# Head-masked X, fp32r rank products and a written TensorE order in the scans of an RWKV-7/gMLP step

## The chip, the core and the metric

The kernel runs on one core of one Trainium2 chip. The metric is the device time of one execution in microseconds (us): the median of three runs before the change is 3405.29 (3395.33 to 3405.65). Times in the text beside it come from one profiled execution of the kernel before.

## The reference

One inference layer of a flow-matching backbone over 640 tokens of width 2048 (128 of context, 512 of a latent grid): adaLN modulation, w_in, on half of the channels a bidirectional RWKV-7 scan and on the other half a chunked gMLP, w_out, a SwiGLU feed-forward network (FFN) and a last RMSNorm. What the change touches is this:

```python
def _delta_scan(r, w, k, v, aa, bb, s0, reverse):
    def step(S, inp):
        r_t, w_t, k_t, v_t, a_t, b_t = inp
        sa = jnp.einsum('bhvk,bhk->bhv', S, a_t)
        S = S * w_t[:, :, None, :] + sa[..., None] * b_t[:, :, None, :] + v_t[..., None] * k_t[:, :, None, :]
        return S, jnp.einsum('bhvk,bhk->bhv', S, r_t)
...
    wt = jnp.tanh(wd)
    for d in range(2):
        w_log = -jax.nn.softplus(-(lp['w0'][d] + wt @ lp['w2'][d])) - 0.5
        decay = heads(jnp.exp(-jnp.exp(w_log)))
        a = jax.nn.sigmoid(lp['a0'][d] + ad @ lp['a2'][d])
        kd = heads(k * (1.0 + (a - 1.0) * lp['k_a']))
        y, s_fin = _delta_scan(rh, decay, kd, vh, -kk, kk * heads(a), s0[:, d], reverse=(d == 1))
        out = out + _group_norm(y, lp['gn_w'], lp['gn_b']) \
            + jnp.sum(rh * kd * lp['r_k'], axis=-1, keepdims=True) * vh
    o = out.reshape(B, T, D_A) * gate
...
    x = x + g1 * (jnp.concatenate([o_a, o_b], axis=-1) @ lp['w_out'])
```

There are 16 heads of 64 channels, two directions d, and a rank of 64 for `wt @ w2` and `ad @ a2` (the rank products).

## The kernel before, in words

Channels lie on the 128 partitions, tokens along the free axis in two halves of 320 (HALF). Every large product is made in fp32r, in three passes: each operand is split into a rounded part hi and a remainder lo, and hi x hi, hi x lo and lo x hi are added up in one PSUM bank (`win` L185 to L187, `wout` L999 to L1001, w_out's first half L1382 to L1384). `split` (L163 and L164) makes hi on ScalarE and lo on VectorE from each weight block of 128x512 that SP's queue has loaded.

The first long stage multiplies h by w_in, block by block. Generators ride between its passes, with budgets that a `Mixer` hands out: for each of eight pairs of heads `take_r`, `take_v` and `take_k`. `take_k` prepares the scan in chunks of 64 tokens, ten per direction. Its rank products (pwa, L562) are plain fp32 matmuls of 64 rows: wl holds w2 in the lower and a2 in the upper 64 partitions, and wa holds tanh(wd) and ad likewise (`low_rank`, L483 and L484). From the decays and keys VectorE makes R and X (X in four operations, L606 to L610); pG (L624) multiplies X by R for each chunk and head in fp32, 64 rows a head, the two heads in turn. The transposes pXT (L641), the first W (pW0, L652) and `solve` with its blocks of 32x32 follow. w_mod's products (pm, L869) run in the same stage. Everything that the scans need goes through DRAM (d_S).

The second stage holds the scans. w_out's second half (`wout_b`) needs only the gMLP's output and gives TensorE something to do: eight of its 32 blocks come first, the rest lies between the scans' steps. A hop is a turn of a loop (117 in all); pair p starts at hop 13p (OFF), and two pairs are under way at a time. `recur(p)` takes one yield a phase, three phases a step: w (L1117) and the outputs y of the step ahead (L1083, L1088), then u (L1132), then s (L1153), from which VectorE makes the new state SN (L1157 to L1160). Each is four small matmuls for each of two chains (latent and context), in a bank of its own for each chain: two banks for w, s and swap, one for u, two for y, from which ScalarE copies Y with its sum (L1102). `finish(p)` then normalises Y over the heads (GpSimd L1182 and L1192), joins the two directions by matmuls with I and J (pO, L1200) and applies the gate (pmm, L496); a second Mixer deals it out in pieces. On every engine the instructions stand in the order that the scheduler picks, from the order of the code and its own costs.

After the scans, w_out's first half runs through 16 blocks for each half of the tokens, in two banks of pbig and two of pb2 in turn, each block with its eight row blocks of o on end. The FFN follows.

Of the kernel before, what the change touches and what calls it, by code (L numbers as in the profile page):

```python
# [10 lines left out]
F32 = mybir.dt.float32  # L11
# [8 lines left out]
P = 128  # L20
# [31 lines left out]
LAG = 4  # L52
LAST_LAG = 3
ROWO = 4
RAWB = 13
WTAIL = 8
OFF = 13
MB = 6
# [26 lines left out]
def flow_step(ctx: ExitStack, tc, x_prompt, x_sample, state_rwkv, c, c_ctx, w_mod, b_mod,  # L85
# [279 lines left out]
    wa = bk.tile([P, T], F32, name="wa", bufs=1)  # L365
# [132 lines left out]


# [25 lines left out]
    def take_k(pr, p):  # L525
# [26 lines left out]
        for d in range(2):  # L552
# [5 lines left out]
            for hf in range(2):  # L558
                s = slice(HALF * hf, HALF * hf + HALF)
                two = [pk.tile([P, HALF], F32, tag="g", name="pwa") for _ in range(2)]  # L560
                for h in range(2):
                    TE.matmul(two[h], wl[hsl(h), d, :], wa[hsl(h), s], start=True, stop=True)  # L562
# [42 lines left out]
            X = bz.tile([P, NCH, 2, CH], F32, tag="X", name="X", bufs=1)  # L605
            V.tensor_mul(rev(X[0:64, :, 1, :]), v3(tha)[0:64], i3[0:64])  # L606
            V.tensor_mul(rev(X[64:128, :, 0, :]), v3(tha)[64:128], i3[64:128])
            yield 1.5
            V.tensor_mul(rev(X[0:64, :, 0, :]), v3(f)[0:64], i3[0:64])
            V.tensor_mul(rev(X[64:128, :, 1, :]), v3(f)[64:128], i3[64:128])  # L610
# [8 lines left out]
            for (c0, c1) in ((0, 4), (4, 8), (8, NCH)):  # L619
                two = [pk.tile([P, 4, P], F32, tag="g", name="pG") for _ in range(2)]  # L620
                for cc in range(c0, c1):
                    for h in range(2):
                        s = hsl(h)
                        TE.matmul(two[h][:, cc - c0, :], X[s, cc, :, :].rearrange("p s t -> p (s t)"),  # L624
                                  R[s, cc, :, :].rearrange("p s t -> p (s t)"), start=True, stop=True)
# [10 lines left out]
            for (c0, c1) in ((0, 8), (8, NCH)):  # L636
                two = [pk.tile([P, 8, CH], F32, tag="g", name="pXT") for _ in range(2)]
                for cc in range(c0, c1):
                    for h in range(2):
                        s = hsl(h)  # L640
                        TE.transpose(two[h][:, cc - c0, :], X[s, cc, :, :].rearrange("p s t -> p (s t)"), ident[s, s])  # L641
# [373 lines left out]
    with ExitStack() as ph:  # L1015
        rw = ph.enter_context(tc.tile_pool(name="rw", bufs=1))
        sm = ph.enter_context(tc.tile_pool(name="sm", bufs=2))
        pws = ph.enter_context(tc.tile_pool(name="pws", bufs=2, space=PSUM))
        pu = ph.enter_context(tc.tile_pool(name="pu", bufs=1, space=PSUM))
# [32 lines left out]

        def swap(src):
            ps = pws.tile([P, 2, CH], F32, tag="ws", name="swap")
            for d in range(2):
                for h in range(2):
                    TE.matmul(ps[hsl(h), d, :], src[hsl(h), d, :], I2[hsl(h), :], start=True, stop=True)
            o = sm.tile([P, 2, CH], F32, tag="ST", name="ST", bufs=7)
            V.tensor_copy(o, ps)
            return o  # L1060

        def recur(p):
# [7 lines left out]
            yield 1  # L1070
            late = []

            def outputs():
                if not late:
                    return


                ys = [py.tile([P, 2, CH], F32, tag=f"y{d}", name="y_ps") for d in range(2)]

                def states(e, r, ST, **kw):  # L1080
                    for d in range(2):
                        for h in range(2):
                            TE.matmul(ys[d][hsl(h), e, :], r[hsl(h), d, F_R + CH:F_R + P], ST[hsl(h), d, :], **kw)  # L1083

                def chunk(e, r, **kw):
                    for d in range(2):
                        for h in range(2):
                            TE.matmul(ys[d][hsl(h), e, :], r[:, d, F_G + CH * h:F_G + CH * h + CH],  # L1088
                                      r[:, d, F_Z + CH * h:F_Z + CH * h + CH], **kw)

                for e, (cc, r, ST) in enumerate(late):
                    if ST is None:
                        chunk(e, r, start=True, stop=True)
                    elif e == 0:
                        states(e, r, ST, start=True, stop=False)
                        chunk(e, r, start=False, stop=True)
                    else:
                        chunk(e, r, start=True, stop=False)
                        states(e, r, ST, start=False, stop=True)
                for e, (cc, r, ST) in enumerate(late):  # L1100
                    for d in range(2):
                        S.activation(u.Y[:, d, cc[d], :], ys[d][:, e, :], AF.Copy, accum_out=u.ys[:, d, cc[d]:cc[d] + 1])  # L1102
# [3 lines left out]
            for step in range(len(LATC)):  # L1106
                act = [c for c in chains if step < len(seqs[c[0]])]
                Ws = []
                for ctx_, ST in act:
                    r = recs[p, ctx_, step]  # L1110
# [3 lines left out]
                    w_ps = pws.tile([P, 2, CH], F32, tag="ws", name="w_ps")  # L1114
                    for d in range(2):
                        for h in range(2):
                            TE.matmul(w_ps[osl(h), d, :], r[hsl(h), d, F_R:F_R + CH], ST[hsl(h), d, :],  # L1117
                                      start=True, stop=True)
                    W = sm.tile([P, 2, CH], F32, tag="W", name="W", bufs=4)
                    for h in range(2):  # L1120
                        q = osl(h)
                        V.tensor_add(W[q], w_ps[q], r[q, :, F_Z + CH * h:F_Z + CH * h + CH])
                    Ws.append(W)
                outputs()
                yield 1
                for (ctx_, ST), W in zip(act, Ws):
                    r = recs[p, ctx_, step]
                    ups = pu.tile([P, 2, CH], F32, tag="u", name="u_ps")
                    for d in range(2):
                        for h in range(2):  # L1130
                            q = osl(h)
                            TE.matmul(ups[q, d, :], r[q, d, F_T:F_T + CH],  # L1132
                                      r[q, d, F_Z + CH * h:F_Z + CH * h + CH] if W is None else W[q, d, :],
                                      start=True, stop=True)
                    V.tensor_copy(r[0:64, :, F_Z + CH:F_Z + P], ups[0:64])
                    S.copy(r[64:128, :, F_Z:F_Z + CH], ups[64:128])
                yield 1
                for ch in act:
                    ctx_, ST = ch
                    cc = seqs[ctx_][step]  # L1140
                    r = recs.pop((p, ctx_, step))
                    late.append((cc, r, ST))
                    if step + 1 == len(seqs[ctx_]) and not ctx_:
                        continue
                    s_ps = pws.tile([P, 2, CH], F32, tag="ws", name="s_ps")
                    SN = sm.tile([P, 2, CH], F32, tag="ST", name="SN", bufs=7)
                    ge = gend[:, p].rearrange("p d c -> p (d c)")[:, flip(cc)].unsqueeze(2)
                    if ST is not None:
                        SG = sm.tile([P, 2, CH], F32, tag="SG", name="SG", bufs=4)
                        V.tensor_tensor(out=SG, in0=ST, in1=ge.to_broadcast([P, 2, CH]), op=ALU.mult)  # L1150
                    for d in range(2):
                        for h in range(2):
                            TE.matmul(s_ps[hsl(h), d, :], r[:, d, F_X + CH * h:F_X + CH * h + CH],  # L1153
                                      r[:, d, F_Z + CH * h:F_Z + CH * h + CH], start=True, stop=True)
                    for d in range(2):
                        if ST is None:
                            V.tensor_scalar_mul(SN[:, d, :], s_ps[:, d, :], ge[:, d])  # L1157
# [756 lines left out]
```

## Time and profile before

| what | us |
|---|---|
| median of three runs | 3405.29 |
| the profiled execution | 3410.02 |
| its span | 3408.2 |
| modulation and the first blocks (0 to 150) | 150 |
| w_in with rank products, pG, solve (150 to 1203) | 1053 |
| first blocks of w_out's second half (1203 to 1242) | 39 |
| scans (1242 to 1537) | 295 |
| the last pair's normalisation (1537 to 1560) | 23 |
| w_out's first half (1560 to 1690) | 130 |
| FFN and the end (from 1690) | 1718 |

The stages are read from the first and last instruction of their matmul lines, to a microsecond or so. The profile gives for each engine the time in which it worked, and for TensorE the clock that was granted (1.00 is full). PE is TensorE's matmuls, PEld its weight loads, DVE VectorE, ACT ScalarE, POOL GpSimd, SP the engine that issues most DMAs. A matmul's shape reads rows in use * columns in use. The profiled execution was 4.7 us longer than the median.

### The profile page before, as it was taken

The numbers are of one execution on the slowest core, as the hardware profiler recorded it, in microseconds if no ns is written. First come the engines' busy times: TensorE is split into PE (matmuls) and PEld (weight loads), VectorE is DVE, ScalarE is ACT, GpSimd is POOL, SyncE is SP. The second block draws the span as 40 slices with busy tenths as digits, with TensorE's granted clock in tenths as the row PEclk, the third lists the DMA queues.
The fourth block names the chain that finished last, engine by engine and source line by source line (L and its number), as shares of the span: only waits on it lengthen the run. The fifth ranks groups of instructions, "written<-read, shape, count | busy, mean of one in ns | idle before, by whom it ended". The sixth has DMA issues, their size and how long they took to land.

```text
span 3408.2 us, 72541 instructions
## 1 busy us (share of the span) xinstructions
PE 3249.5 (95%) x28216; PEld 2934.2 (86%) x28216; DVE 2411.4 (71%) x4320; ACT 1450.7 (43%) x3161; POOL 1263.0 (37%) x1112
## 2 busy tenths in 40 slices
PE   6899999999999999998899999999999999999996
PEld 3688777777877887777889999999999999999996
DVE  4547666756866766664887777777777787877787
ACT  3334443433434434333564444444444445443365
POOL 0001122111212103322336565656656555555543
PEclk8999999889999999999999999999999999999998
DMA  8766776566677677654543434344343455543553
GB/s 321 233 188 185 184 189 170 154 171 179 186 186 180 170 226 231 209 163 145 173 124 103 130 114 122 114 126 122 111 123 121 129 165 165 158 138 115 154 163 115
DMA packets 736208, 550.11 MB, mean 161 GB/s; under 512 B 140360, under 2 KB 670040, under 8 KB 727032
## 3 DMA queue, kind: packets, MB, share of 16 engines
q1 hardware_dynamic: 723544, 531.78, 52.5%
q0 software_dynamic: 9984, 13.13, 1.8%
q8 instruction: 222, 3.64, 0.4%
q14 instruction: 122, 1.00, 0.1%
q10 hardware_dynamic: 2336, 0.57, 0.1%
HBM read 436.68 MB, written 111.28 MB: 161 GB/s over the span
## 4 chain that ended last, share of the span: by engine, by line
PE 76%; DVE 11%; issue 4%; DMA 4%; POOL 2%; ACT 2%; SPq 0%; DVEq 0%; ACTq 0%; POOLq 0%
PE P L1529 15%; PE P L1527 14%; PE P L1528 14%; PE big L185 4%; PE big L187 4%; PE big L186 4%; PE pG L624 3%; PE pm L869 2%; PE big L999 2%; DMA raw<-in_w_in_dram 1%; DVE lo L1330 1%; DMA wt<-in_w_mod_dram 1%; PE big L1382 1%; PE big L1384 1%; PE pmm L496 1%
## 5 line engine op out<-in xcount | busy, mean ns | idle before, releaser
L1529 PE MATMUL P<-xo,lo 128*128 128x320 f32 x2352 | 728.1, 310 | 2.3 <-DVE lo L1330 2.2
L1527 PE MATMUL P<-xo,hi 128*128 128x320 f32 x2352 | 727.8, 309 | 1.8 <-ACT hi L1329 1.8
L1528 PE MATMUL P<-xo,hi 128*128 128x320 f32 x2352 | 727.7, 309 | 0.0
L1330 DVE TENSOR_TENSOR lo<-raw,hi 128x512 fp32r<-128x512 f32 x532 | 502.7, 948 | 179.1 <-ACT hi L1329 174.3
L1329 ACT CAST hi<-raw 128x512 fp32r<-128x512 f32 x532 | 330.7, 622 | 496.5 <-PE P L1528 395.1
L185 PE MATMUL big<-h_hi,hi 128*128 128x320 f32 x1376 | 458.2, 333 | 7.8 <-ACT h_hi L341 4.0
L1529 PEld LDWEIGHTS P<-xo,lo 128*128 128x128 f32 x2352 | 442.5, 188 | 3.0 <-DVE lo L1330 3.0
L187 PE MATMUL big<-h_hi,lo 128*128 128x320 f32 x1376 | 444.2, 323 | 0.7 <-DVE lo L164 0.7
L186 PE MATMUL big<-h_lo,hi 128*128 128x320 f32 x1376 | 443.7, 322 | 0.9 <-DVE h_lo L342 0.9
L1527 PEld LDWEIGHTS P<-xo,hi 128*128 128x128 f32 x2352 | 442.7, 188 | 2.0 <-ACT hi L1329 2.0
L1528 PEld LDWEIGHTS P<-xo,hi 128*128 128x128 f32 x2352 | 442.5, 188 | 0.0
L1440 POOL TENSOR_TENSOR raw<-raw 128x512 f32<-128x512 f32 x252 | 407.6, 1627 | 14.9 <-DVE lo L1330 3.3
L1529 PE MATMUL P<-xd,lo 128*128 128x320 f32 x1232 | 383.3, 311 | 14.1 <-DVE lo L1330 13.7
L1527 PE MATMUL P<-xd,hi 128*128 128x320 f32 x1232 | 381.8, 310 | 4.2 <-ACT hi L1329 1.9
L1528 PE MATMUL P<-xd,hi 128*128 128x320 f32 x1232 | 380.7, 309 | 0.0
L164 DVE TENSOR_TENSOR lo<-raw,hi 128x512 fp32r<-128x512 f32 x268 | 185.7, 695 | 243.1 <-ACT hi L163 217.7
L185 PEld LDWEIGHTS big<-h_hi,hi 128*128 128x128 f32 x1376 | 268.4, 195 | 84.0 <-issue 56.9
L163 ACT CAST hi<-raw 128x512 fp32r<-128x512 f32 x268 | 165.4, 619 | 292.4 <-PE big L186 143.1
L186 PEld LDWEIGHTS big<-h_lo,hi 128*128 128x128 f32 x1376 | 268.6, 195 | 17.4 <-issue 11.8
L187 PEld LDWEIGHTS big<-h_hi,lo 128*128 128x128 f32 x1376 | 268.2, 195 | 12.2 <-issue 4.8
L1329 ACT CAST hi<-rawd 128x512 fp32r<-128x512 f32 (+1 forms) x288 | 168.9, 588 | 244.6 <-PE P L1528 207.7
L1529 PEld LDWEIGHTS P<-xd,lo 128*128 128x128 f32 x1232 | 231.2, 188 | 20.4 <-DVE lo L1330 20.3
(362 smaller groups left out, 6303.3 us busy)
## 6 DMA issues: line engine op xcount, KB each, us to landing
wt<-in_w_mod_dram SPq DMA_DIRECT2D x96, 1024.0 KB
raw<-in_w_ffn_gate_dram SPq DMA_DIRECT2D x182, 256.0 KB
raw<-in_w_ffn_up_dram SPq DMA_DIRECT2D x182, 256.0 KB
rec<-d_S SPq DMA_DIRECT2D x80, 576.0 KB
raw<-in_w_in_dram SPq DMA_DIRECT2D x172, 256.0 KB
rawd<-in_w_ffn_down_dram SPq DMA_DIRECT2D x128, 256.0 KB
raw<-in_w_out_dram SPq DMA_DIRECT2D x96, 256.0 KB
xd<-d_os SPq DMA_DIRECT2D x66, 320.0 KB
```

The costliest lines, as they stand in the source:

```text
L163: S.copy(hi, raw)
L164: V.tensor_sub(lo, raw, hi.bitcast(F32))
L185: TE.matmul(halves[hf], hi[:, k, :], h_hi[:, kb, s], start=(kb == 0), stop=False)
L186: TE.matmul(halves[hf], hi[:, k, :], h_lo[:, kb, s], start=False, stop=False)
L187: TE.matmul(halves[hf], lo[:, k, :], h_hi[:, kb, s], start=False, stop=(kb == KB - 1))
L624: TE.matmul(two[h][:, cc - c0, :], X[s, cc, :, :].rearrange("p s t -> p (s t)"), R[s, cc, :, :].rearrange("p s t -> p (s t)"), start=True, ...
L1329: S.copy(hi[:, 0:nk], raw[:, 0:nk])
L1330: V.tensor_sub(lo[:, 0:nk], raw[:, 0:nk], hi[:, 0:nk].bitcast(F32))
L1440: G.tensor_tensor(out=o[:, 0:nk], in0=p[:, 0:nk], in1=q[:, 0:nk], op=ALU.subtract)
L1527: TE.matmul(ps, hi[:, k, :], xk[:, 0, :], start=f, stop=False)
L1528: TE.matmul(ps, hi[:, k, :], xk[:, 1, :], start=False, stop=False)
L1529: TE.matmul(ps, lo[:, k, :], xk[:, 0, :], start=False, stop=l)
```

## The change

1. **Rank products.** wa gets a second plane, in fp32r: tanh(wd) and ad rounded in the one head's rows, their remainder in the other rows. The weights are loaded into both halves, and a rounded part wh and a remainder wr are made of them. Two fp32r passes over 128 rows then take the place of one fp32 matmul over 64.
2. **pG.** XZ is one tile with a plane for each head, in which the other head's rows are zero; they are set once. pG then runs over 128 rows for each head. The transposes still take 64.
3. **Scans.** One pool of four banks serves w, u, s and swap, both chains in one bank; y has one bank. The state part of y (`states`) stands apart from the chunk part (`outputs`). `recur` has six yields a step and is called twice a hop, so a step still takes three hops. `norm`, `join` and `gate` take `finish`'s place at fixed hops. Inside `manual_schedule` TensorE's instructions stand in the order of the code. Two blocks (FRONT) of w_out's second half come first in place of eight, three (REST) stay behind the loop.
4. **w_out's first half.** For the first six blocks (AHEAD) the part with o's first four row blocks comes ahead of all else; pb2 gets four banks.
5. The scratch for dynamic DMA is set to 4096.

```diff
+AHEAD = 6
-WTAIL = 8
+FRONT = 2
+REST = 3
+LATE = 2
-MB = 6
...
-    wa = bk.tile([P, T], F32, name="wa", bufs=1)
+    wa = bk.tile([P, 2, T], F32R, name="wa", bufs=1)
...
-            S.activation(wa[0:64, :], z[0:64, :], AF.Tanh)
-            S.copy(wa[64:128, :], z[64:128, :])
+            S.activation(z[0:64, :], z[0:64, :], AF.Tanh)
+            for i, (s, o) in enumerate(((hsl(0), hsl(1)), (hsl(1), hsl(0)))):
+                S.copy(wa[s, i, :], z[s, :])
+                V.tensor_sub(wa[o, i, :], z[s, :], wa[s, i, :].bitcast(F32))
...
+    XZ = bz.tile([P, NCH, 2, 2, CH], F32, name="XZ")
+    for h in range(2):
+        G.memset(XZ[hsl(h), :, 1 - h], 0.0)
...
-        wl = bk.tile([P, 2, P], F32, tag="wl", name="wl", bufs=1)
-        nc.sync.dma_start(wl[0:64, :, :], w2[0, :, :, p * P:(p + 1) * P].rearrange("d k n -> k d n"))
-        nc.sync.dma_start(wl[64:128, :, :], a2[0, :, :, p * P:(p + 1) * P].rearrange("d k n -> k d n"))
+        wr, wh = (bk.tile([P, 2, 2, P], F32R, tag=n, name=n, bufs=1) for n in ("wr", "wh"))
+        wl = bk.tile([P, 2, 2, P], F32, tag="t1", name="wl", bufs=2)
+        for i, w in enumerate((w2, a2)):
+            for h in range(2):
+                nc.sync.dma_start(wl[hsl(h), i], w[0, :, :, p * P:(p + 1) * P].rearrange("d k n -> k d n"))
         yield from shifted(zk, pr, 8 + p)
+        S.copy(wh, wl)
+        V.tensor_sub(wr, wl, wh.bitcast(F32))
...
-                    TE.matmul(two[h], wl[hsl(h), d, :], wa[hsl(h), s], start=True, stop=True)
+                    TE.matmul(two[h], wh[:, h, d, :], wa[:, h, s], start=True, stop=False)
+                    TE.matmul(two[h], wr[:, h, d, :], wa[:, h, s], start=False, stop=True)
...
-                        TE.matmul(two[h][:, cc - c0, :], X[s, cc, :, :].rearrange("p s t -> p (s t)"),
-                                  R[s, cc, :, :].rearrange("p s t -> p (s t)"), start=True, stop=True)
+                        TE.matmul(two[h][:, cc - c0, :], XZ[:, cc, h, :, :].rearrange("p s t -> p (s t)"),
+                                  R[:, cc, :, :].rearrange("p s t -> p (s t)"), start=True, stop=True)
...
-        pws = ph.enter_context(tc.tile_pool(name="pws", bufs=2, space=PSUM))
-        pu = ph.enter_context(tc.tile_pool(name="pu", bufs=1, space=PSUM))
+        pws = ph.enter_context(tc.tile_pool(name="pws", bufs=4, space=PSUM))
...
+        def bank(name):
+            return pws.tile([P, 2, 2, CH], F32, tag="ws", name=name)
...
+            def states():
...
+                ys = py.tile([P, 2, 2, CH], F32, tag="y", name="y_ps")
...
-                outputs()
-                yield 1
+                ys = states()
+                yield
+                outputs(ys)
+                yield
+                ups = bank("u_ps")
...
+                yield
+                yield
+                yield
+                s_ps, go = bank("s_ps"), []
...
-        m3.add(wout_b(), 8.0 + 16 * 7.2)
-        m3.run(4.0 + 8 * 4.0)
+        m3.add(wout_b(), 8.0 + 16 * 6.4)
+        m3.run(4.0 + FRONT * 3.2)
...
-            for p, gen in list(act):
-                if next(gen, None) is None:
-                    act.remove((p, gen))
-                    m2.finish(p - 1)
-                    m2.add(finish(p), 18.0)
-                m3.run(m3.left / max(1, 2 * (hops - hop - WTAIL)))
-            m2.run(m2.left / MB)
+        with tc.manual_schedule(engines={mybir.EngineType.PE}):
+            for hop in range(hops):
...
+                for p, gen in act:
+                    next(gen)
+                for job in list(after):
+                    if job[0] < 0:
+                        next(job[2], None)
+                    elif job[0] in (LATE, LATE + 1):
+                        join(job[1], job[0] - LATE)
+                for p, gen in list(act):
+                    if next(gen, 0) == 0:
+                        act.remove((p, gen))
+                        after.append([-7, p, norm(p)])
...
+                m3.run(max(0.0, m3.left - REST * 3.2) / (hops - hop))
...
-        pb2 = ph.enter_context(tc.tile_pool(name="pb2", bufs=2, space=PSUM))
+        pb2 = ph.enter_context(tc.tile_pool(name="pb2", bufs=4, space=PSUM))
...
+        for m in range(AHEAD):
+            four_blocks(0, m, 0)
         for hf in range(2):
             s = slice(HALF * hf, HALF * hf + HALF)
             for m in range(KB):
...
+                if hf or m >= AHEAD:
+                    four_blocks(hf, m, 0)
+                ps = four_blocks(hf, m, 1)
...
-    nc = _bacc.Bacc("TRN2", target_bir_lowering=False, num_devices=1)
+    nc = _bacc.Bacc("TRN2", target_bir_lowering=False, num_devices=1, dynamic_dma_scratch_size=4096)
```

`four_blocks(hf, m, q)` makes the twelve passes of block m with row blocks 4q to 4q + 3 of o, into a bank that q = 0 opens and q = 1 closes.

How this moves TensorE's instructions is seen best at two places. The first is the first pair's first rank product in the w_in stage (big is a product with w_in; h_hi and h_lo are the parts of the normalised x). Before:

```order
667 L185 MATMUL big<-h_hi,hi 128x320
668 L186 MATMUL big<-h_lo,hi 128x320
669 L187 MATMUL big<-h_hi,lo 128x320
670 L562 MATMUL pwa<-wa,wl 128x320 x2
671 L185 MATMUL big<-h_hi,hi 128x320
```

Now:

```order
669 L189 MATMUL big<-h_hi,lo 128x320
670 L574 MATMUL pwa<-wa,wh 128x320
671 L575 MATMUL pwa<-wa,wr 128x320
672 L574 MATMUL pwa<-wa,wh 128x320
673 L575 MATMUL pwa<-wa,wr 128x320
674 L187 MATMUL big<-h_hi,hi 128x320
```

The two matmuls of 64 rows became four of 128 at the same place; pG's rows keep their places too.

The second place is in the middle of the scans on TensorE (big is a product of w_out's second half; s_ps, u_ps, w_ps and y_ps are the steps of the pairs under way). Before:

```order
5226 L1153 MATMUL s_ps<-rec 64x64 x8
5227 L999 MATMUL big<-oh,hi 128x320
5228 L1000 MATMUL big<-ol,hi 128x320
5229 L1001 MATMUL big<-oh,lo 128x320
5230 L1132 MATMUL u_ps<-W,rec 64x64 x4
5231 L999 MATMUL big<-oh,hi 128x320
5232 L1000 MATMUL big<-ol,hi 128x320
5233 L1001 MATMUL big<-oh,lo 128x320
5234 L999 MATMUL big<-oh,hi 128x320
5235 L1000 MATMUL big<-ol,hi 128x320
5236 L1001 MATMUL big<-oh,lo 128x320
5237 L1117 MATMUL w_ps<-SN,rec 64x64 x8
```

Now:

```order
5210 L1142 MATMUL u_ps<-W,rec 64x64 x8
5211 L1169 MATMUL s_ps<-rec 64x64 x4
5212 L1010 MATMUL big<-oh,hi 128x320
5213 L1011 MATMUL big<-ol,hi 128x320
5214 L1012 MATMUL big<-oh,lo 128x320
5215 L1010 MATMUL big<-oh,hi 128x320
5216 L1011 MATMUL big<-ol,hi 128x320
5217 L1012 MATMUL big<-oh,lo 128x320
5218 L1122 MATMUL w_ps<-SN,rec 64x64 x4
5219 L1095 MATMUL y_ps<-SN,rec 64x64 x4
5220 L1105 MATMUL y_ps<-rec 64x64 x4
5221 L1169 MATMUL s_ps<-rec 64x64 x8
```

The small matmuls of a hop stand together in two groups with the big products between them, where before big products stood between s and u and between u and w.

More of the change, by code (lines that the diff above doesn't have):

```diff
@@ L1177, in finish @@
-            u = U[p]
             for d in range(2):
@@ L1207, in finish @@
[L1207 to L1214 removed]
+                for (a, b) in HV:
+                    G.tensor_tensor(out=y[:, a:b], in0=y[:, a:b], in1=bc(ys[:, a:b], b - a), op=ALU.mult)
@@ new lines, in gate @@
+        def gate(p, hf):
+            u = U[p]
+            s = slice(HALF * hf, HALF * hf + HALF)
+            ps = po.tile([P, HALF], F32, tag="g", name="pmm")
+            for i, (l, r) in enumerate(((u.g2a, gs1), (u.g2b, gs2))):
+                TE.matmul(ps, l, r[:, s], start=(i == 0), stop=(i == 1))
+            V.scalar_tensor_tensor(out=u.bv[:, s], in0=u.bv[:, s], scalar=gb2[:, p:p + 1],
+                                   in1=ps, op0=ALU.add, op1=ALU.mult)
+            if hf:
+                nc.sync.dma_start(d_o[p], u.bv)
+                dump(f"o{p}", u.bv)
```

241 lines of the change are left out of this document (125 added, 116 removed).

## Prediction, made before the changed kernel had run

> **What bounds the kernel now.** I read the page from the top: the busy line, then the chain of work that ended last.
>
> ```profile
> span 3408.2 us, 72541 instructions
> ...
> PE 3249.5 (95%) x28216; PEld 2934.2 (86%) x28216; DVE 2411.4 (71%) x4320; ACT 1450.7 (43%) x3161; POOL 1263.0 (37%) x1112
> ...
> PE 76%; DVE 11%; issue 4%; DMA 4%; POOL 2%; ACT 2%; SPq 0%; DVEq 0%; ACTq 0%; POOLq 0%
> ```
>
> TensorE (PE) is busy for 95% of the span and carries 76% of the chain. A change can gain only where it shortens TensorE's own work, lifts its clock, or fills what little idle time it has. The next view, windows by stage (span, busy time of PE, PEld, DVE, ACT, POOL with instruction counts, granted clock, DMA share, GB/s), shows where the change lies: w_in with the rank products and pG to 1203, the scans to 1537, the last pair's normalisation to 1560, w_out's first half to 1690.
>
> ```profile
> core 0: us, PE busy (x) PEld busy (x) DVE busy (x) ACT busy (x) POOL busy (x), PEclk, DMA share, GB/s
> 150.00:1203.00 1053.00, 1011.29 (x10790) 830.10 (x10789) 699.64 (x1395) 436.82 (x943) 192.85 (x305) 0.94 0.66 176
> ...
> 1242.00:1537.00 295.00, 294.56 (x4352) 223.81 (x4350) 192.51 (x634) 101.19 (x475) 74.55 (x98) 1.00 0.66 202
> 1537.00:1560.00 23.00, 13.39 (x118) 9.61 (x117) 6.19 (x12) 3.64 (x10) 11.02 (x14) 0.78 0.19 59
> 1560.00:1690.00 130.00, 119.29 (x767) 114.28 (x767) 91.31 (x179) 61.69 (x114) 39.88 (x38) 0.99 0.56 167
> ```
>
> In the w_in stage TensorE lacks two things: 42 us of idle time (1053 less 1011) and clock. A mean of 0.94 over 1053 us is 63 us of lost time. The scans have no idle time at all (294.6 of 295), so there only the count and cost of TensorE's own steps can shrink. Everything behind 1690 is untouched.
>
> **Rank products.** The matmul timeline around one set of pwa (start, duration, shape, records) is this; an fp32 matmul leaves two records.
>
> ```profile
> 208.60 0.30 PE L187 MATMUL big<-h_hi,lo 128*128 128x320 f32 x1
> 208.83 0.81 PE L562 MATMUL pwa<-wa,wl 64*128 64x320 f32 x4
> 209.57 0.41 PE L185 MATMUL big<-h_hi,hi 128*128 128x320 f32 x1
> 209.82 0.30 PE L186 MATMUL big<-h_lo,hi 128*128 128x320 f32 x1
> ...
> 210.99 0.31 PE L185 MATMUL big<-h_hi,hi 128*128 128x320 f32 x1
> ```
>
> The eight steps from 209.82 to 210.99 give 0.147 us for one fp32r product of this size. The set costs 0.74 us, and on each side a start comes late: 208.83 follows 208.60 by 0.23 (0.08 over a step), 209.82 follows 209.57 by 0.25 (0.10 over). That is 0.92 us. After, four fp32r passes on 128 rows are the same shape as their neighbours: 4 x 0.147 = 0.59. With 128 records (row below) there are 32 sets: 32 x 0.33 = **-11 us**.
>
> ```profile
> L624 PE MATMUL pG<-R,X 64*128 64x128 f32 x640 | 101.3, 336 | 20.3 <-DVE X L606 15.9 <-DVE GA L632 2.7 <-DVE X L610 0.8
> ...
> L562 PE MATMUL pwa<-wa,wl 64*128 64x320 f32 x128 | 33.8, 481 | 1.6 <-ACT tha L565 1.3 <-ACT sg L565 0.2
> ```
>
> **pG.** Its 640 records stay; only the rows in use go from 64 to 128. Three groups of now, and an fp32 matmul on 128 rows of the same width (psp) as the price of after:
>
> ```profile
> 227.84 1.50 PE L624 MATMUL pG<-R,X 64*128 64x128 f32 x16
> 229.27 0.42 PE L186 MATMUL big<-h_lo,hi 128*128 128x320 f32 x1
> ...
> 1084.91 1.16 PE L624 MATMUL pG<-R,X 64*128 64x128 f32 x8 [1.72 <-DVE X L606]
> 1085.99 1.02 PE L869 MATMUL pm<-wt,cT 128*2 128x512 f32 x2
> 1086.94 2.41 PE L624 MATMUL pG<-R,X 64*128 64x128 f32 x16
> 1089.29 0.42 PE L187 MATMUL big<-h_hi,lo 128*128 128x320 f32 x1
> ```
>
> ```profile
> 1165.60 1.41 PE L738 MATMUL psp<-wspT,vt 128*128 128x128 f32 x10
> 1166.77 0.39 PE L185 MATMUL big<-h_hi,hi 128*128 128x320 f32 x1
> ```
>
> The groups take 1.43 + 1.08 + 2.35 = 4.86 us for 40 records, and a change of array shape adds 0.17 each (priced under the scans): 5.37. At psp's 1.17 / 10 = 0.117 they would take 4.68. So -0.69 per 40 records, **-11 us** over 640. A cross-check from the order of the instructions: matmuls whose rows and columns in use differ from the one ahead fall from 649 to 482 in this stage, and 167 x 0.17 is -28 for pwa and pG together; that is the lower end. The dearer end is +37, worked out under the rivals.
>
> The Trainium skill ("TensorEngine Tiling (Array Packing)", Theoretical Speedup) speaks against this part: with at most 64 rows in use, two tiles work side by side, up to twice as fast, and this is given up. The rows don't bear it out so far: 0.122 per record on 64 rows against 0.117 on 128.
>
> **Clock.** The granted clock falls to half in stretches of this stage. First pG's own part in three of them (PE and PEld busy, clock, DMA share, GB/s), then all of the longest:
>
> ```profile
> 442.90:456.60 13.70, 6.74 (x32) 5.86 (x31) 0.50 0.75 167
> 617.00:644.30 27.30, 7.45 (x32) 6.27 (x32) 0.50 0.57 145
> 777.40:780.80 3.40, 0.00 (x0) 0.00 (x0) 0.51 0.19 61
> ```
>
> ```profile
> 617.00:644.30 27.30, 25.92 (x253) 21.98 (x253) 16.89 (x43) 9.18 (x22) 6.19 (x11) 0.50 0.57 145
> ```
>
> The long ones contain 32 pG records, the one without any lasts 3.4 us. In the longest TensorE is busy for 25.92 of 27.30 us and still at half. I take it that work on 64 rows holds the clock down once an idle moment has dropped it, and that on 128 rows it comes back sooner: about a third of the 63 us, **-22** (ends 0 and -63). The drop itself stays, since the wait for X ahead of pG stays (20.3 us of idle time in pG's row).
>
> The Trainium skill ("TensorE: Matmul & The Clock Gate", Part 1) has the full clock back after about 3.4 us of sustained work. The stretch of 27.3 us disagrees. By that rule alone the edit would leave the clock as it is: a rival below.
>
> **What comes late next.** The three terms take 44 us from TensorE's work in a stage where VectorE (DVE) already makes it wait for X. Some of it becomes waiting. VectorE is busy for 699.64 of 1053 us, so I charge a fifth, **+9** (ends 0 and +44). Stage: **-35**.
>
> **New operations in the stage.** Each pair gets a ScalarE copy (wh), a VectorE subtraction (wr) and two more SP loads; low_rank gets four small ones; XZ's zeros are set once on GpSimd. By the nearest rows (both 128x512):
>
> ```profile
> L163 ACT CAST hi<-raw 128x512 fp32r<-128x512 f32 x161 | 99.4, 619 | 155.3 <-PE big L186 140.5 <-DMA raw<-in_w_in_dram 10.8 <-issue 2.0
> ```
>
> ```profile
> L164 DVE TENSOR_TENSOR lo<-raw,hi 128x512 fp32r<-128x512 f32 x161 | 110.2, 686 | 188.4 <-ACT hi L163 163.0 <-ACT XT L645 17.1 <-PE pmm L496 5.0
> ```
>
> 8 x 0.62 and 8 x 0.69 us lie under w_in's matmuls: both rows show idle time ten times that. I take 0; uncovered 10. The loads lie ahead of other loads in SP's queue at a DMA share of 0.66, and wl now holds one of two "t1" buffers until wh and wr are made, early in the pair: 0. The smaller DMA scratch: 0.
>
> **Scans.** The price of a change of array shape:
>
> ```profile
> 1304.41 0.45 PE L1153 MATMUL s_ps<-rec 128*64 128x64 f32 x8
> 1304.79 0.42 PE L999 MATMUL big<-oh,hi 128*128 128x320 f32 x1
> ...
> 1309.11 0.69 PE L1153 MATMUL s_ps<-rec 128*64 128x64 f32 x16
> 1309.73 0.41 PE L999 MATMUL big<-oh,hi 128*128 128x320 f32 x1
> ...
> 1310.37 0.34 PE L1200 MATMUL pO<-I,Y 64*64 64x64 f32 x4
> ```
>
> Eight records take 0.38, sixteen 0.62: 0.03 each and 0.14 fixed. Three big products take 0.64 where three steps are 0.44: 0.20 fixed. A round trip is 0.34, one change 0.17. The order has 559 changes between the first swap and the last gate product before and 349 after: 210 x 0.17 = **-36**. The number of matmuls is the same.
>
> The fixed order adds waits. In the 117 hops, w of a step stands behind s of the step ahead and needs SN, which VectorE makes:
>
> ```profile
> 1309.61 0.86 DVE L1159 SCALAR_TENSOR_TENSOR SN<-s_ps,gend,SG 128x64 f32<-128x64 f32 x4 [0.25 <-PE s_ps L1153]
> ```
>
> SN starts 0.50 us after s; half of its 0.86 serves one state, so the first is there about 0.9 and both 1.36 us after s. Between them now stand six big products (6 x 0.147 + 0.20 = 1.08) and mostly a u or s (0.38). That covers it but for a little. Behind a waiting w on TensorE stand y, the other pair's u and the big products; VectorE's W and ScalarE's Y wait for those. Only four hops lack big products. The y bank is single now; ScalarE empties it in four times 0.42 us (rows below), of 7.6 us that a step of three hops lasts (295 / 117 x 3). I take **+8** for both (ends 0, and +60 if 0.5 us stayed open in every hop). Scans: **-28**.
>
> ```profile
> L1102 ACT ACTIVATE Y<-y_ps 128x64 f32<-128x64 f32 x158 | 33.8, 222 | 49.0 <-PE y_ps L1088 41.6 <-PE y_ps L1083 6.9
> L1102 ACT ACTIVATION_READ_ACCUMULATOR Y<-y_ps 128x1 f32 x158 | 31.6, 202 | 0.0
> ```
>
> **The end of the scans.** Here TensorE stands idle behind the last pair's normalisation on GpSimd (POOL):
>
> ```profile
> 1545.33 0.39 PE L1200 MATMUL pO<-I,Y 64*64 64x64 f32 x2 [4.27 <-POOL Y L1192]
> ...
> 1549.14 0.36 PE L1200 MATMUL pO<-J,Y 64*64 64x64 f32 x1 [3.42 <-POOL Y L1192]
> ```
>
> GpSimd's chain is unchanged, and now as then some w_out products stand in between; three blocks held back fill a little more: **-2** (ends -7 and +4). Behind it, w_out's first half waits for its weights' remainder:
>
> ```profile
> PE big L1384 <- DVE lo L164: 7.3, 5, 3.8
> ```
>
> Six blocks now start on o's first half, four blocks of banks deep; that hides only a start: **-2** (ends -8 and +4).
>
> **Sum.** -35 - 28 - 2 - 2 = -67. The profiled execution took 3410.0 us (2 around its span): 3343. The median shown is 4.7 lower, 3405.3; on its scale the forecast is **3338**.
>
> **Rivals**, each on that scale.
> - *The clock gains nothing.* For: the drops are short where TensorE has only other work behind an idle moment, and the idle moments stay. Against: the long stretches. 3338 + 22 = **3360**. This is the case that the Trainium skill's page "TensorE: Matmul & The Clock Gate" would expect.
> - *The clock comes back whole.* For: most stretches hold pG. Against: the one that holds none. 3338 - 41 = **3297**.
> - *VectorE takes TensorE's place in the w_in stage.* For: 15.9 of pG's 20.3 idle us are put down to its X. Against: 699.64 of 1053 busy. All 44 become waits: 3338 + 35 = **3373**.
> - *pG's two heads run side by side on 64 rows now.* pG on 128 rows costs 640 x 0.117 = 75 us; side by side it would cost half, 37, now: +37 in place of -11, **3386**. For: the group at 227.84 takes 0.089 a record. Against: the three together take 0.122. This is the case of the Trainium skill's page "TensorEngine Tiling (Array Packing)".
> - *Slower: the fixed order waits in every hop* (s, SN, w), where the scheduler's own order put other work. The rest of the sum gains 75, so it decides from 75 / 117 = 0.64 us a hop; at 1.0 us it costs 117 in place of 8: **3447**. For: SN takes up to 1.36 us and nothing may overtake. Against: 1.08 us of big products stand there.
> - *No effect*: the scans' time is another resource's and the w_in stage's is DVE's: **3405**. Against: 294.56 of 295 busy.
>
> **How the numbers follow.** Forecast 0.45, clock nothing 0.13, clock whole 0.12, VectorE 0.12, side by side 0.03, slower 0.10, no effect 0.05. The range leaves out the last two: **3290 to 3395**, from the whole clock with a little of the other lower ends to the side-by-side rival with some of the waits. A measurement tells 0.3% from no change: faster 0.85, within 0.3% 0.05, slower 0.10.
>
> **What would show it.** After: pwa in 0.59 us a set between neighbours at full step; pG near 0.117 a record and no half-clock stretch of over 10 us; a mean clock of about 0.96 in the w_in stage, ending 35 us sooner; scans of about 267 us, still without idle time. Wrong if idle time ahead of pG grows by more than 20 us, if w waits for SN by over 0.2 us a hop, or if the half-clock stretches keep their length.

## The result, and the profile after

The changed kernel takes 3354.75 us (median of 4 runs, 3349.06 to 3357.39), the kernel before beside it 3404.62: 50 us less, a ratio of 0.9858 (95% interval 0.9837 to 0.9879). Measured once more, beside other runs, the ratio was 0.9829 (0.9804 to 0.9854, run e9 below). The forecast was 3338.

The page of the changed kernel, the same three lines as of before:

```profile
span 3355.6 us, 72549 instructions
...
PE 3174.8 (95%) x28216; PEld 2917.9 (87%) x28216; DVE 2431.7 (72%) x4338; ACT 1452.6 (43%) x3170; POOL 1265.9 (38%) x1114
...
PE 74%; DVE 11%; issue 6%; DMA 5%; POOL 3%; ACT 2%; SPq 0%; DVEq 0%; POOLq 0%; ACTq 0%
```

TensorE has 75 us less to do, but the span is only 53 shorter, and in the chain DMA, GpSimd and the issue of instructions have grown. The windows by stage say where. First the kernel before, cut at the last product of w_in (1202.3), the first w (1242.1) and the last y (1537.6); the columns are those of the prediction's windows.

```profile
150.00:1202.30 1052.30, 1010.59 (x10784) 829.40 (x10783) 699.46 (x1394) 436.12 (x942) 192.59 (x305) 0.94 0.66 176
1202.30:1242.10 39.80, 38.40 (x270) 35.75 (x269) 25.24 (x59) 15.03 (x32) 1.45 (x2) 1.00 0.85 269
1242.10:1537.60 295.50, 295.06 (x4360) 224.15 (x4359) 192.77 (x633) 101.09 (x476) 74.55 (x98) 1.00 0.66 201
```

Then the changed kernel at the same events:

```profile
150.00:1156.30 1006.30, 959.66 (x10793) 816.61 (x10793) 701.39 (x1404) 437.05 (x950) 198.22 (x305) 0.98 0.68 185
1156.30:1197.50 41.20, 20.56 (x103) 17.30 (x101) 19.35 (x35) 10.95 (x20) 1.67 (x2) 0.67 0.77 250
1197.50:1473.20 275.70, 272.11 (x4448) 223.47 (x4447) 195.50 (x648) 102.97 (x483) 77.12 (x98) 1.00 0.69 214
```

The middle row is the surprise. Between w_in and the scans TensorE has 103 matmul records in place of 270 and takes as long: it is idle for half of the time and runs at 0.67 of its clock. To compare like with like, the products of w_out have to be counted in the trace, because the change moves them: 54 in place of 192 ahead of the scans, 637 in place of 583 in the scans, 845 in place of 761 behind them, at 0.147 us each.

| stage | before | after | moved products | like for like | forecast |
|---|---|---|---|---|---|
| w_in, 150 to its last product | 1052.3 | 1006.3 | 0 | **-46** | -35 |
| from there to the first w | 39.8 | 41.2 | -20.3 | **+22** | 0 |
| scans, first w to last y | 295.5 | 275.7 | +7.9 | **-28** | -28 |
| last y to the last sum of squares | 152.6 | 160.1 | +12.3 | **-5** | -4 |
| FFN and the end | 1717.8 | 1722.3 | 0 | +4 | 0 |

The sum is -53, the difference of the spans. The last row is within what that stage, which the change doesn't touch, varies by among the runs here (1718 to 1726).

The lines that the prediction named come out as follows. A set of rank products in the timeline:

```profile
210.07 0.31 PE L189 MATMUL big<-h_hi,lo 128*128 128x320 f32 x1
210.22 0.31 PE L574 MATMUL pwa<-wa,wh 128*128 128x320 f32 x1
...
210.66 0.31 PE L575 MATMUL pwa<-wa,wr 128*128 128x320 f32 x1
210.81 0.31 PE L187 MATMUL big<-h_hi,hi 128*128 128x320 f32 x1
```

Four passes take 0.59 us (210.22 to 210.81), and neither side loses anything. pG's row in the w_in stage:

```profile
L635 PE MATMUL pG<-R,XZ 128*128 128x128 f32 x640 | 91.6, 286 | 15.8 <-DVE XZ L618 11.5 <-DVE GA L643 2.7 <-DVE XZ L621 1.5
```

Idle time ahead of it fell from 20.3 to 15.8 us; over the stage idle time rose from 42 to 47. The scans' waits are small, which disposes of the rival that the fixed order waits in every hop (TensorE's idle time in the scans rose from 0.4 to 3.6 us):

```profile
PE w_ps L1122 <- DVE SN L1177: 1.1, 2, 0.6
```

Two waits of w for SN, 1.1 us in all, in 117 hops.

### The profile page after: what moved, and what is told of

Its sections match the earlier page's. It is cut to its first block, busy times and chain, and to the rows that moved or that the text cites. A ratio compares the mean times of both kernels' runs of the same rounds, so it can differ in the third digit from the quotient of the medians.

```text
span 3355.6 us, 72549 instructions
## 1 busy us (share of the span) xinstructions
PE 3174.8 (95%) x28216; PEld 2917.9 (87%) x28216; DVE 2431.7 (72%) x4338; ACT 1452.6 (43%) x3170; POOL 1265.9 (38%) x1114
## 4 chain that ended last, share of the span: by engine, by line
PE 74%; DVE 11%; issue 6%; DMA 5%; POOL 3%; ACT 2%; SPq 0%; DVEq 0%; POOLq 0%; ACTq 0%
PE P L1588 15%; PE P L1587 14%; PE P L1586 14%; PE big L187 5%; PE big L189 4%; PE big L188 4%; PE pG L635 2%; PE pm L880 2%; DVE lo L1376 1%; PE big L1010 1%; PE pblk L819 1%; DMA wt<-in_w_mod_dram 1%; DVE lo L166 1%; PE pXT L652 1%; DMA raw<-in_w_in_dram 1%
## 5 line engine op out<-in xcount | busy, mean ns | idle before, releaser
L189 PE MATMUL big<-h_hi,lo 128*128 128x320 f32 x1376 | 436.3, 318 | 2.7 <-DVE lo L166 2.7
L188 PE MATMUL big<-h_lo,hi 128*128 128x320 f32 x1376 | 435.4, 317 | 0.6 <-DVE h_lo L344 0.5
L1499 POOL TENSOR_TENSOR raw<-raw 128x512 f32<-128x512 f32 x252 | 408.9, 1632 | 14.9 <-DVE lo L1376 3.3
```

What stands on the lines that cost most here:

```text
L188: TE.matmul(halves[hf], hi[:, k, :], h_lo[:, kb, s], start=False, stop=False)
L189: TE.matmul(halves[hf], lo[:, k, :], h_hi[:, kb, s], start=False, stop=(kb == KB - 1))
L1499: G.tensor_tensor(out=o[:, 0:nk], in0=p[:, 0:nk], in1=q[:, 0:nk], op=ALU.subtract)
```

## Where the 22 us ahead of the scans come from

Here is TensorE's timeline of that stretch, first in the kernel before. psp, pw and pvt belong to the gMLP's last groups; big at L999, L1010 in the changed kernel, is a product of w_out's second half.

```profile
1203.59 0.40 PE L999 MATMUL big<-oh,hi 128*128 128x320 f32 x1
...
1210.09 0.33 PE L694 MATMUL pw<-ident,wsp 128*128 128x128 f32 x1 [0.59 <-DMA wsp<-in_w_spatial_dram]
...
1221.32 1.38 PE L738 MATMUL psp<-wspT,vt 128*128 128x128 f32 x10 [0.75 <-DVE vt L725]
```

And in the changed kernel:

```profile
1156.18 1.28 PE L749 MATMUL psp<-wspT,vt 128*128 128x128 f32 x10
1164.03 0.45 PE L705 MATMUL pw<-ident,wsp 128*128 128x128 f32 x1 [6.58 <-DMA wsp<-in_w_spatial_dram]
...
1167.88 0.69 PE L1070 MATMUL swap<-I,s 64*64 64x64 f32 x8 [2.34 <-DMA s<-in_state_rwkv_dram]
1174.91 2.47 PE L749 MATMUL psp<-wspT,vt 128*128 128x128 f32 x10 [6.33 <-ACT gq L691]
1177.93 1.06 PE L1262 MATMUL pxT<-ident,x1T 128*128 128x128 f32 x4 [0.55 <-DVE sp L750]
...
1185.00 0.90 PE L1010 MATMUL big<-oh,hi 128*128 128x320 f32 x2 [2.98 <-ACT oh L997]
```

The last group's chain is as long as before, some 19 us from psp to psp, but nothing of w_out lies beside it: the first product starts at 1185, behind the group, where it started at 1203.59 before, ahead of pw. SP's queue shows why. After, the loads of o (ol<-d_o) that the first blocks need, four of the five below, are issued behind the last group's store (d_o<-praw):

```profile
1178.80 0.33 SPq L756 DMA_DIRECT2D d_o<-praw  x1
1179.18 3.77 SPq L996 DMA_DIRECT2D ol<-d_o  x5
```

Before, all four of them were out 54 us ahead of it:

```profile
1165.79 0.34 SPq L985 DMA_DIRECT2D ol<-d_o  x1
1166.66 0.50 SPq L985 DMA_DIRECT2D ol<-d_o  x1
...
1170.22 0.91 SPq L985 DMA_DIRECT2D ol<-d_o  x2
...
1224.56 0.33 SPq L745 DMA_DIRECT2D d_o<-praw  x1
```

**Theory.** The scratch for dynamic DMA lies at the bottom of SBUF. Making it smaller, which gives the room for the rank products' tiles and XZ, moves the pools that are laid out from the bottom down by 12 KB (12288 bytes). The rank products' tiles take up 5632 of these again below bp, the pool that holds the gMLP's tiles among others; XZ lies above it. The pools laid out from the top, o's tiles among them, stay. By the compiler's addresses o's first four pairs (pool oba) lie at bytes 126432 to 146912 of each partition in both kernels. The pool bp begins at 151936 before and at 145280 after. So 1632 bytes are shared. Only the last of oba's eight tiles reaches so far, yet all four loads go late, so it looks as if the whole pool waits for bp's last user. A second overlap is of the same kind: with four banks of pws, the pool po of the x transposes (pxT) moves from PSUM bank 5 to bank 6, which is one of the two that the gMLP's pool has (6 and 7). **Rivals:** two blocks of w_out in front are too few, whatever the loads do; or SP's queue is simply full there. The addresses come from the compiled programs, not from a trace.

## The experiments

Three chips were used; each ratio is to the kernel before on the same chip.

**e1: the scratch alone.** The kernel before, with

```diff
-    nc = _bacc.Bacc("TRN2", target_bir_lowering=False, num_devices=1)
+    nc = _bacc.Bacc("TRN2", target_bir_lowering=False, num_devices=1, dynamic_dma_scratch_size=4096)
```

> The kernel before with the smaller DMA scratch (4096) and nothing else. Theory: the scratch lies at the bottom of SBUF, so every pool that is laid out from the bottom moves down by 12 KB, and the tiles of o for w_out's second half then share bytes with the pool bp of the last gMLP group; their loads wait for that group, and its chain of about 50 us is no longer covered by w_out products. About 20 us slower than before (3425), all of it between the last product of w_in and the first w of the scans, with some 20 us of idle TensorE there. Rival (the front block count alone, two in place of eight, does it): no change, 3405. Second rival (the scratch serves the DMAs themselves): a change in the w_in stage, where most GpSimd DMAs are.

Measured: 3421.78 against 3403.20, ratio 1.0048 (1.0028 to 1.0067). One number that computes nothing costs 16 us by the ratio. The place is right, its form isn't: the scheduler now starts the scans without any block in front, and the loss lies across both stages. From the last product of w_in to the last y:

```profile
1187.60:1542.80 355.20, 344.52 (x4629) 268.56 (x4627) 221.66 (x693) 117.60 (x509) 75.81 (x100) 0.95 0.64 199
```

It takes 355.2 us, 335.3 (39.8 + 295.5) before, for the same products: 20 more, with TensorE idle for 10.7 us (1.8 before) and at 0.95 of its clock (1.00 before). The w_in stage, where the second rival would show, isn't longer (1037.6 us, 1052.3 before).

**e2: only the scans and w_out's first half**, with the old scratch. The changed kernel, with items 1, 2 and 5 undone.

> The changed kernel without the rank products, without XZ and with the old scratch: only the scans and w_out's first six blocks are changed. Theory: scans 28 us of work cheaper, the end some 4, no loss ahead of the scans from the scratch: 3373, up to 3380 since the pxT transposes still wait for the last gMLP group's PSUM bank. Rival (two front blocks in place of eight cost the cover by themselves): 21 us more, 3394.

Measured: 3382.22, ratio 0.9922 (0.9889 to 0.9955), nearer to the theory's 3380 than to the rival's 3394. The stretch ahead of the scans:

```profile
1193.10:1224.60 31.50, 18.19 (x103) 16.14 (x101) 15.38 (x30) 7.33 (x15) 1.47 (x2) 0.67 0.75 245
```

31.5 us for the work that takes 41.2 in the changed kernel: nearly half of the 22 us is gone with the old scratch, the rest isn't the scratch's.

**e3: only the w_in stage and the scratch.** The kernel before, with items 1, 2 and 5.

> The kernel before with the rank products, XZ and the scratch, and the old scans. Theory: w_in stage 46 us shorter as in the changed kernel, and the loss ahead of the scans from the scratch, about 20: 3379. Rival (the loss belongs to the scans' part): 3359.

Measured: 3383.40, ratio 0.9918 (0.9890 to 0.9945). The w_in stage takes 1000.2 us, the stretch and the scans 360.0 (335.3 before): both terms of the theory, in one run.

**e4: pG on 64 rows again**, and **e5: the rank products in one fp32 pass again**, each from the changed kernel, by the diff's own lines backwards.

> The changed kernel with pG on 64 rows again. Theory (work on 64 rows holds the clock at half once it has dropped): half-clock stretches of over 13 us come back, granted clock of the w_in stage back to 0.94 to 0.95; pG 11 us and the clock some 30 us dearer: 3390 to 3396. Rival (the clock came back for another reason, such as other idle moments): clock stays at 0.98 and the time is 3366.

> The changed kernel with the rank products in one fp32 pass of 64 rows again. Theory: 32 sets at 0.33 us, 11 us slower: 3366, with the granted clock of the w_in stage unchanged at 0.98. Rival (these 64-row passes hold the clock down too): 0.96 or less, over 3375. Rival (VectorE sets the pace of the stage, and the new subtraction took time there): no change or faster, 3350.

Measured: e4 3378.41, ratio 0.9917 (0.9889 to 0.9944); e5 3369.38, ratio 0.9896 (0.9864 to 0.9929). The windows of the w_in stage, first e4:

```profile
150.00:1180.50 1030.50, 991.54 (x10792) 830.72 (x10791) 701.72 (x1404) 436.82 (x949) 199.35 (x305) 0.95 0.66 181
```

and e5:

```profile
150.00:1174.80 1024.80, 972.37 (x10784) 806.26 (x10783) 696.10 (x1392) 434.08 (x940) 194.06 (x305) 0.98 0.67 180
```

With pG on 64 rows the clock is back at 0.95; with pwa on 64 rows and pG on 128 it stays at 0.98. So the clock goes with pG, not with every product on 64 rows. The shorter wait ahead of pG isn't the reason. Its row, first in e4, then in e5:

```profile
L633 PE MATMUL pG<-R,X 64*128 64x128 f32 x640 | 98.8, 312 | 14.9 <-DVE X L615 11.5 <-DVE X L618 1.7 <-DVE GA L641 1.3
L628 PE MATMUL pG<-R,XZ 128*128 128x128 f32 x640 | 91.0, 286 | 20.5 <-DVE XZ L611 15.5 <-DVE GA L636 3.2 <-DVE XZ L615 0.8
```

e4 has the short wait of the changed kernel (14.9 us) and the low clock, e5 the long wait of the kernel before (20.5) and the high clock. In the profiles taken here, those with pG on 64 rows have 0.94, 0.96, 0.95 and 0.95 in this stage (before, e1, e2, e4), all ten with 128 rows 0.98. e4's time is less than was expected, since it loses 24 us of the stage and not 35 to 41: the clock loss varies from profile to profile even where this stage's code is the same (0.94 to 0.96 in before, e1 and e2). e5 is a little slower than expected: 18 us of the stage, 12 of them work (1024.8 - 972.37 is 52 us idle, 47 in the changed kernel).

**e6: none of w_out's blocks ahead** (AHEAD = 0, with the choice of bank that goes with it).

> The changed kernel with w_out's first half in the old order of blocks (none ahead; four banks of pb2 stay). Theory: worth the 2 us forecast, 3357 (3355 to 3361). Rival (the blocks ahead cover the last pair's normalisation): about 4 us of idle time more, 3359 to 3363.

Measured: 3348.57 on the chip whose kernel before takes 3396.29, ratio 0.9847 (0.9798 to 0.9896): no difference from the changed kernel that this interval could show. From the last y to the last sum of squares e6 takes 159 us, the changed kernel 160. The blocks ahead are worth nothing that can be seen.

**e7: o's two pools exchanged**, so that the first four pairs no longer touch bp:

```diff
-        o_hi[kb], o_lo[kb] = (obp[kb % 8 // 4].tile([P, T], F32R, tag=f"{n}{kb % 8}", name=n) for n in ("oh", "ol"))
+        o_hi[kb], o_lo[kb] = (obp[1 - kb % 8 // 4].tile([P, T], F32R, tag=f"{n}{kb % 8}", name=n) for n in ("oh", "ol"))
```

> The changed kernel with the two places of o's tiles exchanged, so that the loads of w_out's second half no longer share bytes with the last gMLP group's pool. Theory of the overlap: these loads go early, one block of 24 products goes ahead of the group's last transposes, the rest still waits for the PSUM bank of the x transposes: 4 to 8 us faster, 3347 to 3351. Rival (the loads are late because SP's queue is full): no change, 3355.

Measured: 3338.95, ratio 0.9818 (0.9777 to 0.9860). The loads of o are early again (the last two at 1116.40, 55 us ahead of the last store), and the stretch takes what it takes with the old scratch:

```profile
1148.80:1180.50 31.70, 18.23 (x103) 16.22 (x101) 15.35 (x30) 7.33 (x15) 1.66 (x2) 0.68 0.75 243
```

31.7 us, 31.5 in e2. The edit takes no transfer off SP's queue, so that rival falls, and the shared bytes cost 9.5 us here (41.2 less 31.7). The times agree, though with intervals as wide as the effect: on the same chip e6, as fast as the changed kernel, takes 9.6 us more.

**e8: the bank moved too, and five blocks in front.**

```diff
+        po = ph.enter_context(tc.tile_pool(name="po", bufs=1, space=PSUM))
         pws = ph.enter_context(tc.tile_pool(name="pws", bufs=4, space=PSUM))
-        po = ph.enter_context(tc.tile_pool(name="po", bufs=1, space=PSUM))
```

with e7's line and FRONT = 5.

> As the run with o's tiles exchanged, and the pool of the x transposes opened ahead of the scans' banks, so that it doesn't take the last gMLP group's bank, and five blocks in front in place of two. Theory (tile overlap and bank overlap together make the loss ahead of the scans): most of the 20 us of idle time and of the half clock there goes, 3354.8 less 20 to 30: 3325 to 3335. Rival (two blocks in front are the cause, or the scans wait instead with fewer products between their steps): 3345 to 3360.

Measured: 3334.49, ratio 0.9806 (0.9760 to 0.9851). The run on one chip with the changed kernel (e12) tells it better. po now has bank 2, and bank 6 is the fourth bank of pws.

**e9 to e12: on one chip.** The changed kernel; without the fixed order; e8 with two blocks in front; e8 once more.

> The changed kernel as it is, for comparison on one chip with the next three. All theories: 0.9858 of the time before (0.984 to 0.988).

> The changed kernel with TensorE's order in the scans left to the scheduler; banks, states and phases as changed. In its order the array's shape changes 418 times in the scans, where it is 349 with the written order and 559 before. Theory (the number of changes, at 0.17 us each, is what the scans' part buys): 69 changes more, 12 us slower over the front and scans together (about 3367), and still 24 us of work below the scans before. Rival (the written order itself, by having each wait covered, is what gains): scans back near 300 us with visible idle time, 3375 or more. Rival (the written order costs waits): faster than the changed kernel.

> The run with o's tiles exchanged and the bank moved, with two blocks in front as in the changed kernel in place of five. Theory (two blocks are 8 us of cover; the last gMLP group's chain is longer): some 8 to 12 us of idle time ahead of the scans, against 1.6 with five; 5 to 10 us slower than the run with five, 3335 to 3345 by the before of 3405. Rival (the scans' own steps fill the gap): as fast as with five.

> The run with o's tiles exchanged, the bank moved and five blocks in front again, beside the changed kernel on one chip. Theory: 18 to 22 us below the changed kernel (the idle time of 20.6 and the clock of 13.7 us ahead of the scans, less what the scans lose with fewer products between their steps). Rival (the difference seen so far lay in the clock of the w_in stage by chance): within 8 us of it.

| run | us | ratio (95%) |
|---|---|---|
| e9, as changed | 3348.01 | 0.9829 (0.9804 to 0.9854) |
| e10, `if True:` for the manual schedule | 3351.56 | 0.9843 (0.9815 to 0.9871) |
| e11, both overlaps gone, FRONT = 2 | 3333.34 | 0.9793 (0.9769 to 0.9816) |
| e12, both overlaps gone, FRONT = 5 | 3335.00 | 0.9787 (0.9764 to 0.9810) |

The window from the last product of w_in to the last y, which holds 691 products of w_out in all four, is in e9

```profile
1152.20:1467.60 315.40, 291.51 (x4550) 239.37 (x4548) 214.75 (x682) 113.55 (x502) 78.71 (x100) 0.96 0.70 220
```

in e10

```profile
1143.40:1459.20 315.80, 300.03 (x4549) 245.12 (x4547) 213.08 (x682) 113.01 (x502) 77.45 (x100) 0.97 0.70 220
```

in e11

```profile
1144.50:1445.70 301.20, 288.13 (x4549) 237.91 (x4548) 213.11 (x680) 112.02 (x500) 78.69 (x100) 0.98 0.73 228
```

and in e12

```profile
1153.40:1452.40 299.00, 291.70 (x4550) 239.73 (x4548) 211.81 (x680) 112.05 (x500) 78.38 (x100) 0.98 0.73 229
```

Both overlaps together cost 14 to 15 us (315.4 less 301.2 in the window, 3348.0 less 3333.3 in the time): e11 differs from the changed kernel by two lines and loses nothing in the scans. Ahead of the scans its stretch shrinks to 25.0 us. So of the 22 us the tiles cost 9.5, the bank 6.7 (31.7 less 25.0, one profile each), and the 5 or 6 that are left go with two blocks in front.

Five blocks in place of two take these last us (27.7 us of that stretch, with 126 products), but the scans, which have 72 products fewer between their steps, give most of it back. So the rival of the block count holds for that small part of the stretch and falls for the time: e12 is no faster than e11, which was expected to be 5 to 10 us slower. e12 lies 13 us below e9, between the 18 to 22 of its theory and the 8 of its rival.

e10 missed its expectation, and for an instructive reason. Its work is dearer as forecast: 8.5 us more of busy TensorE at a better clock. With the clock taken out that was lost while TensorE was busy (5.5 us in e9, 3.5 in e10) it is 286 against 297 us, some 10.5 more for 69 more changes of shape, which is 0.15 each. But its scheduler starts the first pair's steps beside the last gMLP group, and so wins back in idle time (15.8 us, 23.9 in e9) what it loses in work. The fixed order gains by the changes of shape that it saves, and it gave most of that away ahead of the scans. That an array asked for another shape pays for it is what the Trainium skill says in "TensorEngine Tiling (Array Packing)", Key Properties: changing the tiling mode drains TensorE. The traces agree that a change costs time, and give a price that the page doesn't: about 0.15 us. Whether it is by draining, no run shows.

e11 and e12 beat both kernels: 2.1% below the kernel before, 0.4% below the changed one.

## Why the prediction was right, and where it wasn't

The direction and the range were right, and most terms were near. The time came out 17 us above the forecast: 22 were lost at a place that the sum left out, 4 in the last stage, and 11 more than forecast were won in w_in. That the time came so near is in part luck: the surplus in w_in, the sum of terms that were each off, hid half of what was lost ahead of the scans.

- *Rank products, -11.* Right by itself: the set takes 0.59 us and loses nothing at its sides, and undoing it (e5) costs 12 us of work.
- *pG, -11.* About right by itself: undoing it (e4) costs 9 us of work besides the clock. The rival that the two heads run side by side on 64 rows has fallen, since that would have cost 37. At full clock, from one start to the next and without idle time, a record takes 0.126 us before and 0.116 after, near the 0.122 and 0.117 that were read. But the two terms don't add up: TensorE's work in the stage, with idle time and the loss by the clock taken out, is 947 to 953 us in the kernels with both old parts (before, e1, e2) and 933 to 936 with both new ones (after, e3 and e6 to e12), about 16 less where 22 was forecast.
- *Clock, -22.* Undersized: (1 - 0.94) x 1052 = 63 us lost before and 24 after (a clock of 0.976), so 39 in these two profiles. All four profiles with pG on 64 rows lose 50 on average and the ten on 128 lose 22, so some 28 is the better figure. The step's reason stands as far as it goes: it is pG's rows, as e4 and e5 show, and not the wait ahead of pG. Why the rows matter, the runs don't show. The sign "no half-clock stretch of over 10 us" was nearly met: the longest in the changed kernel is 10.2 us, in e7 17.1.
- *Push-back, +9.* Idle time in the stage rose by 5 in this pair; over the other profiles (42 to 45 us with both old parts, 39 to 47 with both new ones) it didn't rise.
- *Scans, -28.* The sum is right because two errors cancel. Like for like, TensorE's work fell by 31 and not 36 (295.06 less 272.11, and 7.9 for the moved products), which is 0.15 for each of 210 changes of shape, as in e10; and idle time rose by 3 and not 8, of which 1.1 are waits for SN.
- *The end, -2 and -2.* -5 in all, but e6 shows that the second term is nothing: the whole came from idle time (20.3 us before, 15.8 after).
- *The rivals.* "The clock gains nothing" falls with the 28 us, "the clock comes back whole" with the 22 that are still lost, and VectorE, which was to turn 44 us into waits, turned at most 5.
- *"The smaller DMA scratch: 0."* This is the step that failed. It was put at nothing without a reason. It is a change of addresses, and addresses decide which tiles wait for which: e1 puts 16 us on it, and e7 and e2, in which o's tiles are free in two different ways, give the same stretch (31.7 and 31.5 us) in place of 41.2.
- *The stretch ahead of the scans was not priced at all.* The prediction's stages went from w_in to the scans as if the 40 us between were fixed. The order of the instructions at this place would have shown it: before, w_out's blocks stand ahead of and between the last gMLP group's matmuls on TensorE, and after, all of them stand behind.

## What to carry to other kernels

When a change resizes anything that is allocated, compare the addresses before and after at each change of phase: a few shared bytes between a new phase's first tiles and an old phase's last pool turn an early load into a late one, and it shows as a queue in which the load stands behind a store. Price the changes of array shape on TensorE, not only its matmuls: here they were the whole gain of the scans. And list every stage of the timeline in the sum, also those that the change doesn't seem to touch.

## What the runs showed of the hardware

The half clock of TensorE comes in steps of 3.4 us and goes with pG's shape: with pG on 64 of 128 rows 4 to 6% of the w_in stage's clock is lost, on 128 about 2%, though a record of pG at full clock takes nearly as long in both (0.126 and 0.116 us). A change of array shape cost about 0.15 us of TensorE's time here. The Trainium skill ("TensorE: Matmul & The Clock Gate", Part 1) has windows of about 3.4 us, which agrees; that one busy window brings the full clock back does not: in the kernel before it stayed at half for 27.3 us with TensorE busy for 25.92 of them.
